# Output products laid into the last heads of two attentions, a gate/up pair ahead of each down product, modulation products spread thinner

## The chip, the cores and the metric

The kernel runs on one core of one Trainium2 chip. The metric is the device time of one execution in microseconds (us); a lower one is better. Three runs of the kernel before took 2721.72, 2729.32 and 2738.30 us, so the median is 2729.32 us. One further execution was profiled, and took 2725.89 us.

The core has a matrix engine (PE, with its weight loads shown apart as PEld), a vector engine (DVE), an activation engine (ACT), GpSimd (POOL) and a sync engine (SP), which here issues DMA transfers. Each has its own list of instructions and goes through it in order; semaphores make one wait for another.

## The reference, cut to what matters

One sequence of 512 tokens, width 1024, float32, goes through two blocks:

```python
# first block, layer 0, then layer 1
hn = modulate(rms_norm(h, norm1_g[l]), sh1, sc1)
mix = chunk_rel_attention(...)  if l == 0 else  mla_attention(...)     # 16 heads each, ends in  o @ wo
h = h + g1[:, None, :] * mix
hn = modulate(rms_norm(h, norm2_g[l]), sh2, sc2)
h = h + g2[:, None, :] * conv_ffn(hn, f_win[l], f_conv_w[l], f_conv_b[l], f_wout[l])

def conv_ffn(hn, win, conv_w, conv_b, wout):        # 1024 -> 2 x 2816 -> 1024
    y = conv_b + sum(up[:, tap:tap + S] * conv_w[tap] for tap in range(3))   # up: hn @ win, padded
    gate, val = jnp.split(y, 2, axis=-1)
    return (jax.nn.silu(gate) * val) @ wout

# second block
h = h + 0.5 * gt1 * swiglu(modulate(rmsnorm(h)), w1_gate, w1_up, w1_down)    # 2816 wide
h = h + gt2 * ((sigmoid(ga) * (ya @ w_proj_a) + sigmoid(gb) * (yb @ w_proj_b)) @ w_out)
h = h + 0.5 * gt3 * swiglu(modulate(rmsnorm(h)), w2_gate, w2_up, w2_down)
```

Every shift, scale and gate (`sh1`, `sc1`, `g1`, ...) is a column of a product silu(c) @ W + b: the "modulation". There are 184 such columns of 128 numbers.

## The kernel before, in words

The activations lie transposed: feature blocks of 128 on the partitions, 512 tokens along the free axis. `self.h` holds the residual as eight tiles of 128x512. A product of float32 accuracy is made of three matmuls in a reduced format: each operand is a high part (`wh`, `uh`) and a low part (`wl`, `ul`), and `mm3` (L328 to L330) adds high times high, high times low, low times high. A weight tile comes through `wload`: a DMA into one of four `wr` buffers, a cast on ACT (L311), a subtraction on DVE (L312). An activation is split in the same way by `split` (L341 on ACT, L342 on DVE). `gemm` takes one tile of weights and a list of split activations, and sums 3 matmuls of 512 columns for each into one bank of PSUM (three banks of tag "g", two of "s", two of "t", one of "o").

A framework's scheduler puts the instructions of each engine in an order. The order in which the code is written is its starting point; it may move a ready instruction ahead of one that it expects to wait. What it lists is what the engine carries out, one after the other.

**Attention** (`heads`, called by `block_a` and by `mla`): 16 heads, each with four query steps. A step makes scores on PE, a softmax on DVE (L477, L479, L721 or L935) and ACT (L478); two steps later it makes transposes on PE (L510) and a split of them (`pth`, `ptl`); after the fourth step the values product follows (`ps_o`, twelve matmuls). During a pair of heads, the projections of the next pair give PE something else to do; for the last heads nothing is left to project. Each finished pair of heads is written to DRAM (`oa`, L565).

**Output product** (`branch_out`): weights of a tail (`tw`), then the pairs back from DRAM and split (`pairs_back`, through two buffers "tn"), then eight blocks: weights `wo[j]` (`bwo[j]` in the second attention), a gemm over the first five pairs (15 matmuls), and on DVE `resid` (L445), which adds it to `h`. A tail over the other three pairs follows in two halves of the tokens, and the norm of the next stage with it.

**FFN** (`ffn`, used by `conv_ffn` twice and by `swiglu` twice): 22 hidden blocks in parts of 8, 8 and 3 (`PARTS`), and 3 for the tail. A hidden block is two gemms of 24 matmuls (the gate and value halves), and then work on ACT and DVE that ends in the split `hidh`, `hidl`. After each part come its eight down products: weights `fout`, a gemm over the part's hidden blocks, `resid`. In the two conv FFNs, four modulation columns are computed after each hidden block from the third on (`run_bg(4)`, `gemv`: a load of 512 KB through the same `wr` ring on SP, a multiplication with a sum on DVE, L462, and an addition, L463). There are 72 of them in each conv FFN.

Of the kernel before, what the change touches and what calls it, by code (L numbers as in the profile page):

```python
# [19 lines left out]
P = 128  # L20
# [264 lines left out]
class _K:  # L285
# [195 lines left out]

    def heads(self, pool, n, begin, lag=2):

        wait = []

# [6 lines left out]
        for h in range(n):  # L495
            probs, v, m, done = begin(h)
            pt = [pool.tile([P, 13, P], F32R, tag=t, bufs=2, name=t) for t in ("pth", "ptl")]
            for i in range(4):
                then = (lambda pt=pt, v=v, m=m, done=done: done(self.values(pt, v, m))) if i == 3 else None
                wait.append((i, probs(i), pt, then))  # L500
                if len(wait) > lag:
                    finish()
        while wait:
            finish()

    def transpose(self, i, p, pt):
# [59 lines left out]

    def pairs_back(self, dram):
        oo = []
        for p in range(8):
            if p < 7:  # L570
                t = self.tmp(tag="tn", bufs=2)
                self.nc.sync.dma_start(t, dram[p])
            else:
                t = self.o32
            oo.append(self.hl(self.gp, "u", 16, t))
        return oo


    def build(self):
# [19 lines left out]
        with self.tc.tile_pool(name="ca", bufs=1) as ca:  # L599
# [11 lines left out]
            with self.tc.tile_pool(name="pr", bufs=1) as pr:  # L611
                norm = self.conv_ffn(0, norm, m0(5), 4, lambda: self.norm_of("kv_norm_g", mk(1), mk(0)),
                                     self.rope_tables(pr))
                cact = self.c_act(ca, 1)
                norm = self.mla(norm, m1)
            self.bg = self.gemv_jobs(cact, [(j, 112, "b_ada") for j in range(112, 184)])
            norm = self.conv_ffn(1, norm, m1(5), 4, lambda: _Norm2(
                self, self.col("final_g", 0, 8), self.gain_scale(ada(1), self.col("g_ff1", 0, 8)), ada(0)))
# [30 lines left out]
    def block_a(self, cact, m0):  # L649
# [4 lines left out]
        with self.tc.tile_pool(name="pa", bufs=1) as pa:  # L654
# [75 lines left out]

            self.heads(pa, 16, begin)
            out = self.branch_out(pa, [("pth", 2), ("ptl", 2)] * 2, od, "wo", m0(2), lambda: self.norm_of("norm2_g0", m0(4), m0(3)))
        self.dump("ha", self.h)
        return out

    def branch_out(self, pool, tags, od, w, gate, mk_norm):

        tw = self.tail_weights(pool, tags, w + "t")
        oo = self.pairs_back(od)
        for j in range(8):  # L740
            x = self.wload(self.a[w][j], HEAD * P)
            self.resid(j, self.gemm(x, oo[:HEAD]), gate[:, j:j + 1])
        norm = mk_norm()
        self.tail(tw, oo[HEAD:], gate, norm)
        return norm


    def two_first(self, pf, ap, u):
# [5 lines left out]
        pss = self.gemm_halves(ws, u, "ggtt")  # L754
        return {0: pss[:2], 1: pss[2:]}

    def conv_ffn(self, l, norm, gate, nbg, mk_norm, aside=None):
# [26 lines left out]

        norm = self.ffn(hidden, f"fout{l}", gate, mk_norm)
        self.dump(f"hf{l}", self.h)
        return norm

    def ffn(self, hidden, wd, gate, mk_norm):
        with self.tc.tile_pool(name="pf", bufs=1) as pf:  # L790
            for pi, (f0, f1) in enumerate(PARTS):
# [3 lines left out]
                if pi == 2:  # L795
                    tw = self.tail_weights(pf, [("tw", 4)] * 4, wd + "t")
                    last = []
                    for f in range(f1, KF):
                        hidden(pf, f, last)
                n, g = f1 - f0, 8 // (f1 - f0)  # L800
                for j in range(8):
                    if j % g == 0:
                        w = self.wload(self.a[f"{wd}{pi}"][j // g], g * n * P)
                    self.resid(j, self.gemm(w, hid, (j % g) * n * P), gate[:, j:j + 1])
            self.run_bg(1000)
            norm = mk_norm()
# [51 lines left out]
    def mla(self, norm, m1):  # L858
        nc, a, gp = self.nc, self.a, self.gp
        with self.tc.tile_pool(name="pm", bufs=1) as pm:  # L860
# [78 lines left out]

            self.heads(pm, 16, begin)  # L940
            out = self.branch_out(pm, [("pth", 2), ("ptl", 2)] * 2, od, "bwo", m1(2), lambda: self.norm_of("norm2_g1", m1(4), m1(3)))
# [4 lines left out]
    def swiglu(self, n, norm, gt, mk_norm):  # L946
# [18 lines left out]

        out = self.ffn(hidden, f"w{n}d", hg, mk_norm)
        self.dump(f"hs{n}", self.h)
# [403 lines left out]
```

## Time and profile before

| | |
|---|---|
| three runs | 2721.72, 2729.32, 2738.30 us |
| the profiled execution | 2725.89 us |
| its span (first to last instruction) | 2724.1 us |
| PE busy | 2599.7 us, 95% |
| PEld busy | 2138.4 us, 79% |
| DVE busy | 1761.2 us, 65% |
| ACT busy | 1208.1 us, 44% |
| granted PE clock, mean | 0.981 of full |

PE is the engine that is busy nearly all the time. A matmul's busy time includes its way through the array, during which the next one has already begun; how fast PE really goes is read from the distance between the starts of two matmuls. The clock granted to PE goes between two levels, 1.2 and 2.4 GHz; the windows give its mean as a share of the higher one.

### The profile page before, as it was taken

Reading aid. Unit: us, or ns where it says so; the run is one execution under the profiler, and the core shown is the slowest. Engines: PE = TensorE matmul, PEld = TensorE weight load, DVE = VectorE, ACT = ScalarE, POOL = GpSimd, SP = SyncE. Lnnn points to the kernel's source line nnn. Section 1 sums busy time; section 2 is a strip of 40 time slices with the busy share of each in tenths; the row PEclk is TensorE's granted clock in tenths of the full one; section 3 lists DMA queues with packets and bytes.
Section 4 is the critical chain, followed back from the end, with each engine's and each line's share of the span. In section 5 each row is a group of like instructions: output and inputs, shape, how many; then the busy total and the mean of one; then the engine's idle time right before and its main releaser. Section 6 shows DMA issues by size and latency. Waiting matters only on the chain. (4 is left out here: it accounts for less than half of the span.)

```text
span 2724.1 us, 34800 instructions
## 1 busy us (share of the span) xinstructions
PE 2599.7 (95%) x12666; PEld 2138.4 (79%) x12666; DVE 1761.2 (65%) x3362; ACT 1208.1 (44%) x2119; POOL 95.2 (3%) x138
## 2 busy tenths in 40 slices
PE   7898999999898999999999999999999989999998
PEld 5776888788676888778888888887877767888887
DVE  7796896867788796958633335788365455533344
ACT  5465542334677442324622224677355434422232
POOL 1000200000000100000100001000000000100000
PEclk9999999999899999999999999999999989999999
DMA  8774376663154465745133332433257653232331
GB/s 275 208 217 132 121 236 204 227 200 114 52 140 132 138 223 173 261 163 180 45 109 93 97 116 76 119 96 97 80 171 264 228 180 124 74 98 93 101 112 43
DMA packets 146639, 395.77 MB, mean 145 GB/s; under 512 B 23954, under 2 KB 28178, under 8 KB 146468
## 3 DMA queue, kind: packets, MB, share of 16 engines
q1 hardware_dynamic: 146468, 393.55, 45.4%
q8 instruction: 100, 1.64, 0.2%
q14 instruction: 71, 0.58, 0.1%
HBM read 341.05 MB, written 26.21 MB: 135 GB/s over the span
## 5 line engine op out<-in xcount | busy, mean ns | idle before, releaser
L329 PE MATMUL ps_g<-ul,wh 128*128 128x512 f32 (+1 forms) x2156 | 835.8, 389 | 15.9 <-POOL ul L401 13.0
L328 PE MATMUL ps_g<-uh,wh 128*128 128x512 f32 (+1 forms) x2156 | 831.1, 388 | 15.7 <-ACT uh L341 10.8
L330 PE MATMUL ps_g<-uh,wl 128*128 128x512 f32 (+1 forms) x2156 | 829.4, 386 | 0.0
L311 ACT CAST wh<-wr 128x1024 fp32r<-128x1024 f32 (+3 forms) x398 | 397.5, 999 | 928.8 <-PE ps_g L329 698.5
L312 DVE TENSOR_TENSOR wl<-wr,wh 128x1024 fp32r<-128x1024 f32 (+3 forms) x398 | 462.2, 1163 | 250.2 <-ACT wh L311 238.3
L328 PEld LDWEIGHTS ps_g<-uh,wh 128*128 128x128 f32 x2156 | 408.1, 190 | 106.7 <-ACT uh L341 13.4
L329 PEld LDWEIGHTS ps_g<-ul,wh 128*128 128x128 f32 x2156 | 410.2, 190 | 100.5 <-POOL ul L401 18.2
L330 PEld LDWEIGHTS ps_g<-uh,wl 128*128 128x128 f32 x2156 | 409.4, 190 | 79.9 <-issue 2.0
L462 DVE CUSTOM_DVE_ANT_0 wr<-wr,cact 128x1024 f32<-128x1024 f32 x184 | 226.0, 1234 | 69.5 <-DMA wr<-mod 69.1
L328 PE MATMUL ps_g<-hidh,wh 128*128 128x512 f32 x608 | 241.3, 397 | 7.1 <-ACT hidh L341 7.1
L330 PE MATMUL ps_g<-hidh,wl 128*128 128x512 f32 x608 | 241.2, 397 | 0.0
L329 PE MATMUL ps_g<-hidl,wh 128*128 128x512 f32 x608 | 240.8, 396 | 0.0
L328 PEld LDWEIGHTS ps_g<-hidh,wh 128*128 128x128 f32 x608 | 115.2, 190 | 35.5 <-ACT hidh L341 8.3
L329 PEld LDWEIGHTS ps_g<-hidl,wh 128*128 128x128 f32 x608 | 115.0, 189 | 27.8 <-DVE hidl L342 0.2
L330 PEld LDWEIGHTS ps_g<-hidh,wl 128*128 128x128 f32 x608 | 115.3, 190 | 27.3
L445 DVE SCALAR_TENSOR_TENSOR h<-ps_g,mods,h 128x512 f32<-128x512 f32 (+1 forms) x112 | 73.0, 653 | 94.6 <-PE ps_g L330 94.2
L445 DVE SCALAR_TENSOR_TENSOR h<-ps_g,hg,h 128x512 f32<-128x512 f32 (+1 forms) x64 | 43.7, 683 | 127.2 <-PE ps_g L330 127.1
L478 ACT ACTIVATE p<-p,st 128x128 f32<-128x128 f32 (+1 forms) x192 | 107.4, 560 | 40.9 <-DVE st L477 40.0
L963 DVE TENSOR_TENSOR cv<-ps_g,cv 128x512 f32<-128x512 f32 x42 | 29.1, 692 | 127.8 <-PE ps_g L330 126.5
L362 POOL TENSOR_TENSOR acc<-acc,sq 128x256 f32<-128x256 f32 x42 | 34.1, 813 | 2014.5 <-ACT sq L361 1335.8
L341 ACT CAST hidh<-cv 128x512 fp32r<-128x512 f32 x88 | 54.6, 620 | 90.4 <-DVE cv L780 83.2
L398 ACT ACTIVATE uh<-tn,mods 128x256 fp32r<-128x256 f32 (+1 forms) x120 | 60.3, 519 | 65.5 <-DVE tn L394 64.8
(380 smaller groups left out, 3981.4 us busy)
## 6 DMA issues: line engine op xcount, KB each, us to landing
wr<-mod SPq DMA_DIRECT2D x184, 512.0 KB, 4.2
wr<-fin SPq DMA_DIRECT2D x88, 512.0 KB, 4.3
wr<-fout SPq DMA_DIRECT2D x32, 512.0 KB, 3.6
wr<-w1g SPq DMA_DIRECT2D x22, 512.0 KB, 3.5
wr<-w1u SPq DMA_DIRECT2D x22, 512.0 KB, 3.5
wr<-w2g SPq DMA_DIRECT2D x22, 512.0 KB, 3.6
wr<-w2u SPq DMA_DIRECT2D x22, 512.0 KB, 3.5
wr<-wqk SPq DMA_DIRECT2D x16, 512.0 KB, 4.4
```

The costliest lines, as they stand in the source:

```text
L311: nc.scalar.copy(h[:, :n], r[:, :n])
L312: nc.vector.tensor_tensor(l[:, :n], r[:, :n], h[:, :n].bitcast(F32), ALU.subtract)
L328: mm(ps, wh, xh, start=start, stop=False)
L329: mm(ps, wh, xl, start=False, stop=False)
L330: mm(ps, wl, xh, start=False, stop=stop)
L341: self.nc.scalar.copy(h, src)
L362: (eng or nc.vector).tensor_tensor(acc[:, cs], acc[:, cs], s[:, cs], ALU.add)
L398: nc.scalar.activation(h[:, cs], t, AF.Identity, bias=sh)
L445: self.nc.vector.scalar_tensor_tensor(self.h[j][:, cs], ps, g, self.h[j][:, cs], ALU.mult, ALU.add)
L462: nc.vector.tensor_tensor_reduce(w, w, cact, 1.0, 0.0, ALU.mult, ALU.add, accum_out=self.mods[:, j:j + 1])
L478: nc.scalar.activation(p[:, :n], p[:, :n], AF.Exp, bias=st[:, 0:1], scale=-1.0, accum_out=st[:, 1:2])
L963: nc.vector.tensor_tensor(t, pss[1], t, ALU.mult)
```

## The change

Three edits.

1. **Output product inside the last heads.** `heads` takes a list of jobs (`fill`) and calls one after each query step of the last two heads. The first job brings back and splits the first five pairs (now through three buffers "acc"), the next seven are blocks 0 to 6 of the output product, and the eighth block comes after the last head. `branch_out` then loads the tail's weights, brings back pairs 5 to 7, and goes on with the tail. This holds for both attentions.
2. **A pair ahead of each down product.** After parts 0 and 1 of each of the four FFNs, the two gemms of the next part's first hidden block are made (into the two "t" banks of PSUM) before the eight down products; their work on ACT and DVE stays where the next part begins.
3. **Modulation spread.** Three columns instead of four after a hidden block, and one after each of the sixteen down products of parts 0 and 1.

```diff
-    def heads(self, pool, n, begin, lag=2):
+    def heads(self, pool, n, begin, lag=2, fill=()):
...
                 wait.append((i, probs(i), pt, then))
                 if len(wait) > lag:
                     finish()
+                if h >= n - 2 and fill:
+                    fill.pop(0)()
         while wait:
             finish()
+        for f in fill:
+            f()
...
-    def pairs_back(self, dram):
+    def pairs_back(self, dram, p0, p1):
...
-                t = self.tmp(tag="tn", bufs=2)
+                t = self.tmp(tag="acc", bufs=3)
...
-                norm = self.conv_ffn(0, norm, m0(5), 4, lambda: self.norm_of("kv_norm_g", mk(1), mk(0)),
+                norm = self.conv_ffn(0, norm, m0(5), 3, lambda: self.norm_of("kv_norm_g", mk(1), mk(0)),
...
-            self.heads(pa, 16, begin)
+            self.heads(pa, 16, begin, fill=self.branch_head(od, "wo", m0(2)))
...
+    def branch_head(self, od, w, gate):
+
+        oo = []
+
+        def block(j):
+            x = self.wload(self.a[w][j], HEAD * P)
+            self.resid(j, self.gemm(x, oo), gate[:, j:j + 1])
+
+        return [lambda: oo.extend(self.pairs_back(od, 0, HEAD))] + [lambda j=j: block(j) for j in range(8)]
+
     def branch_out(self, pool, tags, od, w, gate, mk_norm):
 
         tw = self.tail_weights(pool, tags, w + "t")
-        oo = self.pairs_back(od)
-        for j in range(8):
-            x = self.wload(self.a[w][j], HEAD * P)
-            self.resid(j, self.gemm(x, oo[:HEAD]), gate[:, j:j + 1])
+        oo = self.pairs_back(od, HEAD, 8)
         norm = mk_norm()
-        self.tail(tw, oo[HEAD:], gate, norm)
+        self.tail(tw, oo, gate, norm)
...
+    def pair_early(self, first, ap, u):
+
+        def early(f):
+            first[f] = [self.gemm(w, u, tag="t") for w in [self.wload(x) for x in ap(f)]]
+
+        return early
...
+                else:
+                    early(f1)
                 n, g = f1 - f0, 8 // (f1 - f0)
                 for j in range(8):
                     if j % g == 0:
                         w = self.wload(self.a[f"{wd}{pi}"][j // g], g * n * P)
                     self.resid(j, self.gemm(w, hid, (j % g) * n * P), gate[:, j:j + 1])
+                    if pi < 2:
+                        self.run_bg(1)
```

How the order moves on the engines, at three places. In the rows `ps_s` are scores, `ps_t<-ident,p` transposes, `ps_o` values, `ps_g<-uh,wh` (or `ul`, `wl`) matmuls of a product with weights.

PE, block A, where head 15's scores begin. Before, scores and transposes follow each other with nothing between:

```order
L551 MATMUL ps_s<-k,q 128x512
L510 MATMUL ps_t<-ident,p 128x128 x2
L550 MATMUL ps_s<-k,q 128x128
L551 MATMUL ps_s<-tn,q 128x128
L550 MATMUL ps_s<-k,q 128x256
L551 MATMUL ps_s<-tn,q 128x256
L510 MATMUL ps_t<-ident,p 128x128 x3
L550 MATMUL ps_s<-k,q 128x384
L551 MATMUL ps_s<-tn,q 128x384
```

After, blocks of the output product stand between them:

```order
L328 MATMUL ps_g<-uh,wh 128x512
L329 MATMUL ps_g<-ul,wh 128x512
L330 MATMUL ps_g<-uh,wl 128x512
L555 MATMUL ps_s<-k,q 128x128
L556 MATMUL ps_s<-tn,q 128x128
L515 MATMUL ps_t<-ident,p 128x128 x3
L328 MATMUL ps_g<-uh,wh 128x512
L329 MATMUL ps_g<-ul,wh 128x512
L330 MATMUL ps_g<-uh,wl 128x512
```

Fifteen matmuls of one block now lie between the scores of one query step and those of the next, and the transposes of an earlier step follow the scores; the blocks stood before in one run behind head 15.

DVE, the same place. `ptl` is the split of the transposes, `p,st<-ps_s,b` the first softmax instruction, L721 (L726 after) the scaling. Before:

```order
L479 RECIPROCAL st<-st 128x1
L477 ISA p,st<-ps_s,b 128x384
L477 ISA st 128x1
L721 TENSOR_SCALAR p<-p,st 128x128
L342 TENSOR_TENSOR ptl<-ps_t,pth 128x3x128
L479 RECIPROCAL st<-st 128x1
L477 ISA p,st<-ps_s,b 128x512
L477 ISA st 128x1
L721 TENSOR_SCALAR p<-p,st 128x256
L342 TENSOR_TENSOR ptl<-ps_t,pth 128x4x128
```

After:

```order
L445 SCALAR_TENSOR_TENSOR h_83<-ps_g,mods,h_83 128x512
L477 ISA p,st<-ps_s,b 128x128
L477 ISA st 128x1
L312 TENSOR_TENSOR wl<-wr,wh 128x640
L479 RECIPROCAL st<-st 128x1
L342 TENSOR_TENSOR ptl<-ps_t,pth 128x3x128
L726 TENSOR_SCALAR p<-p,st 128x128
L342 TENSOR_TENSOR ul<-acc,uh 128x512
L445 SCALAR_TENSOR_TENSOR h_84<-ps_g,mods,h_84 128x512
L477 ISA p,st<-ps_s,b 128x256
```

A split of weights (`wl`), a split of a pair (`ul<-acc`) and the addition to `h` (L445) of an output block now stand between the instructions of a softmax; the addition can't begin before PE has finished its block, and the softmax instruction behind it waits for it.

SP, down products of the first conv FFN's first part. `fout` are weights of a down product, `fin` of a hidden block, `mod` of a modulation column. Before:

```order
L308 DMA wr<-fin 128x1024 x2
L461 DMA wr<-mod 128x1024 x4
L308 DMA wr<-fout 128x1024 x8
L308 DMA wr<-fin 128x1024 x2
L461 DMA wr<-mod 128x1024 x4
L308 DMA wr<-fin 128x1024 x2
```

After:

```order
L461 DMA wr<-mod 128x1024 x3
L308 DMA wr<-fin 128x1024 x2
L461 DMA wr<-mod 128x1024 x3
L308 DMA wr<-fin 128x1024 x2
L308 DMA wr<-fout 128x1024
L461 DMA wr<-mod 128x1024
L308 DMA wr<-fout 128x1024
L461 DMA wr<-mod 128x1024
L308 DMA wr<-fout 128x1024
L461 DMA wr<-mod 128x1024
```

One hidden block's `fin` now goes ahead of the `fout` loads, and a modulation load stands between each two of these; all go through the same four `wr` buffers.

## Rows read from the trace of the kernel before

**Rows 1.** The page, part 1: busy us of each engine, share of span, instructions.

```profile
PE 2599.7 (95%) x12666; PEld 2138.4 (79%) x12666; DVE 1761.2 (65%) x3362; ACT 1208.1 (44%) x2119; POOL 95.2 (3%) x138
```

**Rows 2.** Windows: stretch, its length; PE, PEld, DVE, ACT, POOL busy; granted clock; DMA.

```profile
226.40:258.00 31.60, 22.63 (x118) 16.84 (x117) 24.50 (x73) 22.82 (x56) 0.14 (x1) 0.89 0.42 122
258.00:286.00 28.00, 28.00 (x131) 23.31 (x130) 15.91 (x22) 9.05 (x12) 0.00 (x0) 1.00 0.52 174
...
537.00:548.00 11.00, 9.34 (x29) 7.47 (x30) 4.20 (x6) 2.58 (x3) 0.00 (x0) 0.69 0.25 90
```

**Rows 3.** Windows, same columns: the end of the second attention.

```profile
849.00:888.00 39.00, 32.47 (x187) 24.51 (x186) 32.34 (x104) 30.05 (x76) 0.00 (x0) 0.96 0.46 132
888.00:917.00 29.00, 29.00 (x144) 24.67 (x143) 17.95 (x25) 9.53 (x14) 0.00 (x0) 1.00 0.51 167
```

**Rows 4.** Timeline of PE, block A's end: start, duration, instruction, idle before and releaser.

```profile
226.42 0.22 PE L550 MATMUL ps_s<-k,q 128*128 128x128 f32 x1
...
236.02 0.45 PE L328 MATMUL ps_o<-pth,vsh 128*64 128x512 f32 x1 [1.65 <-ACT pth L341]
...
252.09 0.44 PE L328 MATMUL ps_o<-pth,vsh 128*64 128x512 f32 x1 [1.21 <-ACT pth L341]
...
255.49 0.80 PE L328 MATMUL ps_g<-uh,wh 128*128 128x512 f32 x1
...
284.72 0.28 PE L328 MATMUL ps_g<-uh,tw 128*128 128x256 f32 x1
```

**Rows 5.** Timeline of PE, the second attention's end.

```profile
850.48 0.41 PE L510 MATMUL ps_t<-ident,p 128*128 128x128 f32 x2
...
881.30 0.44 PE L328 MATMUL ps_o<-pth,vs 128*64 128x512 f32 x1 [1.21 <-ACT pth L341]
...
885.38 0.60 PE L328 MATMUL ps_g<-uh,wh 128*128 128x512 f32 x1
...
913.62 0.28 PE L328 MATMUL ps_g<-uh,tw 128*128 128x256 f32 x1
```

**Rows 6.** Timeline of PE, first conv FFN, end of its second part.

```profile
534.63 0.39 PE L329 MATMUL ps_g<-hidl,wh 128*128 128x512 f32 x1
538.66 0.80 PE L328 MATMUL ps_g<-hidh,wh 128*128 128x512 f32 x1 [3.64 <-ACT hidh L341]
539.26 0.63 PE L330 MATMUL ps_g<-hidh,wl 128*128 128x512 f32 x1
539.68 0.63 PE L328 MATMUL ps_g<-hidh,wh 128*128 128x512 f32 x1
...
544.60 0.40 PE L329 MATMUL ps_g<-hidl,wh 128*128 128x512 f32 x1
...
548.92 0.39 PE L330 MATMUL ps_g<-hidh,wl 128*128 128x512 f32 x1
```

**Rows 7.** Timeline of PE, second conv FFN, the same place.

```profile
1170.08 0.80 PE L328 MATMUL ps_g<-hidh,wh 128*128 128x512 f32 x1 [3.47 <-ACT hidh L341]
```

**Rows 8.** Groups by line and form: count, busy us, mean ns, idle before.

```profile
L312 DVE TENSOR_TENSOR wl<-wr,wh 128x1024 fp32r<-128x1024 f32 x334 | 408.3, 1223 | 212.5 <-ACT wh L311 201.0
...
L462 DVE CUSTOM_DVE_ANT_0 wr<-wr,cact 128x1024 f32<-128x1024 f32 x184 | 226.0, 1234 | 69.5 <-DMA wr<-mod 69.1
...
L445 DVE SCALAR_TENSOR_TENSOR h<-ps_g,mods,h 128x512 f32<-128x512 f32 x72 | 54.0, 750 | 89.4 <-PE ps_g L330 89.4
...
L312 DVE TENSOR_TENSOR wl<-wr,wh 128x640 fp32r<-128x640 f32 x32 | 26.0, 821 | 8.2 <-ACT wh L311 8.1
...
L342 DVE TENSOR_TENSOR ul<-tn,uh 128x512 fp32r<-128x512 f32 x21 | 14.2, 686 | 4.6 <-ACT uh L341 4.6
...
L341 ACT CAST uh<-tn 128x512 fp32r<-128x512 f32 x21 | 12.9, 618 | 8.3 <-DVE tn L394 4.9 <-DMA tn<-oa 2.1 <-DMA tn<-ob 1.2
```

**Rows 9.** DMA issues of the page: count, size, median us to landing.

```profile
wr<-mod SPq DMA_DIRECT2D x184, 512.0 KB, 4.2
...
wr<-fout SPq DMA_DIRECT2D x32, 512.0 KB, 3.6
```

More of the change, by code (lines that the diff above doesn't have):

```diff
@@ L480, in softmax @@
         return p, st
-    def heads(self, pool, n, begin, lag=2):
-        wait = []
+    def heads(self, pool, n, begin, lag=2, fill=()):
+        wait, fill = [], list(fill)
         def finish():
@@ L565, in pair_out @@
             self.nc.sync.dma_start(dram[p], self.o32)
-    def pairs_back(self, dram):
+    def pairs_back(self, dram, p0, p1):
         oo = []
-        for p in range(8):
+        for p in range(p0, p1):
             if p < 7:
-                t = self.tmp(tag="tn", bufs=2)
+                t = self.tmp(tag="acc", bufs=3)
                 self.nc.sync.dma_start(t, dram[p])
@@ L616, in build @@
             self.bg = self.gemv_jobs(cact, [(j, 112, "b_ada") for j in range(112, 184)])
-            norm = self.conv_ffn(1, norm, m1(5), 4, lambda: _Norm2(
+            norm = self.conv_ffn(1, norm, m1(5), 3, lambda: _Norm2(
                 self, self.col("final_g", 0, 8), self.gain_scale(ada(1), self.col("g_ff1", 0, 8)), ada(0)))
@@ L783, in hidden, with ffn @@
                 self.run_bg(nbg)
-        norm = self.ffn(hidden, f"fout{l}", gate, mk_norm)
+        norm = self.ffn(hidden, self.pair_early(first, ap, u), f"fout{l}", gate, mk_norm)
         self.dump(f"hf{l}", self.h)
         return norm
-    def ffn(self, hidden, wd, gate, mk_norm):
+    def ffn(self, hidden, early, wd, gate, mk_norm):
         with self.tc.tile_pool(name="pf", bufs=1) as pf:
@@ L938, in begin @@
                 return probs, [x[:, :, 64 * e:64 * e + 64] for x in v], 64, lambda ps: self.pair_out(pm, od, p, ps, e)
-            self.heads(pm, 16, begin)
+            self.heads(pm, 16, begin, fill=self.branch_head(od, "bwo", m1(2)))
             out = self.branch_out(pm, [("pth", 2), ("ptl", 2)] * 2, od, "bwo", m1(2), lambda: self.norm_of("norm2_g1", m1(4), m1(3)))
@@ L964, in hidden @@
             hid.append(self.hl(pf, "hid", 24, t))
-        out = self.ffn(hidden, f"w{n}d", hg, mk_norm)
+        out = self.ffn(hidden, self.pair_early(first, ap, u), f"w{n}d", hg, mk_norm)
         self.dump(f"hs{n}", self.h)
```

## The prediction

> **What bounds the kernel now.** I read the page's engine totals first. PE is busy 95% of the span, DVE 65%, ACT 44% [rows 1], so time can only come out of stretches in which PE waits or runs slowly. To find them I read PE's timeline for the distance between starts. In an undisturbed run, 19 matmuls of 512 columns lie between 544.60 and 548.92, so they start 0.227 us apart (0.445 ns a column), though each is shown as 0.39 or 0.40 us busy [rows 6]. After a long wait they start 0.42 us apart (539.26 and 539.68) [rows 6]: PE then runs at the lower of its two clock levels, and the window over that place shows a granted clock of 0.69 [rows 2].
>
> The change touches three kinds of places.
>
> Block A's end: from 226.42, the first score for which no projection is left as cover, to 284.72, the first of the unbroken tail rows, lie 58.3 us [rows 4]. The 235 matmuls that start there have 90,752 columns, which stream in 40.4 us. So 17.9 us are lost, nearly all before the output product begins at 255.49. There PE waits for the split of the transposes (1.65 and 1.21 us in the rows shown), and the window's granted clock is 0.89 [rows 2, 4].
>
> The second attention's end: from 850.48 to 913.62, 63.1 us [rows 5], 290 matmuls with 107,136 columns, 47.7 us. 15.5 us are lost, again nearly all before its output product at 885.38, and on the same split.
>
> The conv FFNs' second parts: PE reaches the down products and waits 3.64 us (first FFN) and 3.47 us (second) for the last hidden block's split [rows 6, 7], and then goes at half rate. From 534.63 to 544.60 are 10.0 us [rows 6]; the 16 matmuls that start in it would have streamed in 16 x 0.228 = 3.6 us: 6.3 us are lost. For the second FFN I take 0.2 us less by its shorter wait, 6.1 us. After the first parts, and in the two swiglus, PE's timeline shows no such wait.
>
> **The change part by part.** No arithmetic of PE goes or comes; instructions are moved.
>
> *Output product inside block A's last heads.* Seven blocks of 15 matmuls, 15 x 0.228 = 3.4 us each, come between query steps. A step's own attention is 1,920 columns on average (scores 640, transposes 320, a quarter of the values 960), 0.85 us; together 4.3 us. What DVE must do in it: the window of 226.40 to 258.00 holds 24.50 us of DVE work [rows 2] for the twelve steps of the last three heads, with the pair splits among it, so under 2.0 us a step; one weight split of 0.82 us and one addition to h of 0.75 us come on top [rows 8], 3.6 us. So DVE fits a step, without much room. Over the stretch as a whole the sum is tighter: DVE is busy 24.50 + 15.91 = 40.4 us between 226.40 and 286.00 [rows 2], and PE's columns ask for 40.4 us too. DVE's work there isn't all needed before the tail, but two engines with equal work and one fixed order each don't overlap without gaps. The bounds: all 17.9 us come back, or nothing does (the waits only change place). At the new junction behind head 15, ACT's copy of the values and its casts of tail weights, DVE's two subtractions of these and the split of the last pair (0.69 us, [rows 8]) stand ahead of the tail: an estimate of 4 us, against one product block and less as cover (3.4 us and under). 1 to 2 us of the loss stay there. For gaps on DVE, and on PE when the first pairs come back from DRAM, I leave 5 us more. Value taken: 11 us, range 6 to 14.
>
> The pairs are brought back by SP, three of them early, since "acc" has three buffers; the weights of the tail come after the blocks' own. The cast `uh` of a pair now stands ahead of a softmax's exponential on ACT. Before, the 21 casts of this form idled 2.1 us in all on loads of pairs [rows 8], which is small.
>
> *The same in the second attention.* The lost time is 15.5 us. DVE has 32.34 + 17.95 = 50.3 us of work in the 68 us from 849 to 917 [rows 3], and PE's streaming is about 52 us there (the 47.7 us above, and what lies on either side): again two nearly equal loads. Heads 12 and the beginning of 13 stay without cover, since the blocks begin in head 13 by the listed order. Value taken: 8 us, range 4 to 12.
>
> *The pair ahead of the down products.* 48 matmuls, 48 x 0.228 = 10.9 us, now stand between the second part's last gemm and its down products. The wait was 3.64 us, so the pair outlasts it three times over, and no slow clock follows. Nothing is added: the same pair is left out later. If the cover failed, it would be because the pair's own weights are late: two subtractions of 1.22 us on DVE [rows 8], behind a backlog. With three modulation products, a hidden block's DVE work falls by 1.23 us [rows 8] and two short instructions, which shrinks that backlog. Value: 5.5 us in each of the two FFNs, range 4 to 6.3. After the first parts and in the swiglus: 0, since nothing was lost there.
>
> *Modulation spread.* It takes work off DVE in the hidden stage (PE streams there for the most part, so little direct gain) and adds it to each of 32 down blocks. Such a block asks DVE for an addition (0.75 us), a weight subtraction (1.22 us) and now a product (1.23 us, all [rows 8]) with its two short instructions, some 3.4 us; PE takes 24 x 0.228 = 5.5 us. Value 0. Bounds: from a gain of 2 us (hidden stages that were a little behind) to a loss that rival C works out.
>
> The sum: 11 + 8 + 5.5 + 5.5 = 30 us. Against the profiled execution of 2725.89 us that gives 2695.9 us. The median of the three runs lies 3.4 us above that execution, and I take half of this difference: 2697.6, in round numbers **2698 us**. Ends of the terms: 6 + 4 + 4 + 4 - 2 = 16 us and 14 + 12 + 6.3 + 6.1 + 2 = 40 us, times of 2712 and 2687 us on the same base.
>
> **The rivals.**
>
> A. DVE and ACT take the place of the waits. On DVE a softmax instruction now stands behind an addition that waits for PE's block, and behind pair and weight splits that wait for a DMA. For it: DVE's 40.4 us against PE's 40.4 [rows 2, 4]. Against: two query steps, 8.6 us, lie between a softmax and its use. Then the attentions give a third of their loss, 17.9/3 + 15.5/3 = 11 us, and with the FFNs' 11 us: 2725.9 - 22 + 1.7 = 2705.5 us. The Trainium skill states a rule that makes this possible (Perfetto Trace Analysis, Tensor Engine Instruction): ACT, DVE and GpSimd are strict FIFO, unlike PE, which can pull weight loads ahead. Where it bites, the trace will show DVE idle on L445 with ready work behind it; the trace of before can't, as no addition stands among the softmaxes there.
>
> B. Only idle time comes back, and half-rate stretches remain for a reason of their own. Idle by busy time is 31.60 - 22.63 = 9.0 us in block A, 39.00 - 32.47 = 6.5 us in the second attention [rows 2, 3], 3.64 and 3.47 us in the FFNs [rows 6, 7]: 22.6 us at most, 2705 us. Against: the slow stretch stands right behind the wait [rows 6]. The Trainium skill (Trainium Kernel Development and Optimization, Performance Expectations) calls matmul busy time a bad metric, because matmuls are pipelined; by that rule B's cap is none. The trace agrees on the rule itself, with 0.39 us busy against 0.227 us from start to start.
>
> C. Slower: the down products wait for weights. A `fout` load lands 3.6 us after its issue, a `mod` load 4.2 us [rows 9], and the products L462 idled 69.1 us on their loads, 0.38 us for each of 184 [rows 8]. In the down stage the loads now alternate in one ring of four, and a buffer comes free only when DVE has done with it: if DVE waits for a `mod`, the next block's weights wait behind it. If each of the 32 blocks in the conv FFNs came 1 us late, that is 32 us and cancels the gain; from there on the change is slower: at 1.5 us late, 48 - 30 = 18 us lost, 2746 us. Against: two loads for 5.5 us are no higher rate than the six for 10.9 us (48 matmuls) of a hidden block before, and a lead of about two buffers, 11 us, stands against 4.2 us of landing, a cast, and a subtraction of 1.22 us.
>
> D. The change doesn't do what it says where it counts: the waits in the heads come from the scheduler's list, which shifts in earlier heads too, and what is gained in the last heads is lost there. Then only the FFN terms are left, 2725.9 - 11 + 1.7 = 2716.6 us.
>
> **How the numbers follow.** Forecast (2687 to 2702) 0.55; A and B together 0.30 (A 0.22, B 0.08), 2702 to 2711; D 0.10, 2711 to 2722; C 0.05. The range takes in the forecast's lower end with some room for a larger gain, and reaches up through A and B into D: 2682 to 2712. A measurement of this kernel can tell 0.5%, 13.6 us, from no change: faster means below 2715.7 us. Forecast, A, B and a third of D lie there: 0.88. The rest of D and a C that stops near 1 us: 0.08. C beyond: 0.04.
>
> **What would show it.** In the changed kernel's profile: block A from the first score without cover to the tail in 46 to 49 us where 58.3 stood; no wait above 1 us on the split of transposes there, and a granted clock near 1.00; no gap before the first `hidh` matmul of a second part, but 48 starts of a gate/up pair (`ps_t`) 0.23 us apart; in the down products starts 0.23 us apart throughout. Wrong if PE's waits in the heads are now on `wh`, `uh` or `wl` (A), if starts stay 0.42 us apart without a wait before them (B), or if the down stage shows a wait for `wh` or `wl` in every block (C).

## The result and the profile after

The changed kernel took 2696.31 us (median of 4 runs, 2693.35 to 2701.35) against 2729.23 us before (median of 4). The ratio is 0.9877, with a 95% interval of 0.986 to 0.9894: 33 us faster. 2698 us were forecast. The profiled execution of it took 2697.24 us, 28.7 us less than that of before. Timed a second time it gave 2692.13 us, ratio 0.9864 (0.9846 to 0.9882).

The page's engine totals, which answer to [rows 1] (busy us, share of the span, instructions):

```profile
PE 2587.6 (96%) x12666; PEld 2125.6 (79%) x12666; DVE 1756.0 (65%) x3362; ACT 1204.9 (45%) x2118; POOL 90.8 (3%) x138
```

PE is busy 12 us less and the span is 28.6 us shorter; the instructions are as many, but for one load of a table on ACT (2118 for 2119).

The ends of the two attentions as windows (the columns of [rows 2]):

```profile
216.50:262.80 46.30, 43.67 (x230) 34.84 (x230) 32.98 (x84) 26.20 (x59) 0.14 (x1) 1.00 0.47 136
829.50:883.50 54.00, 52.30 (x286) 42.00 (x285) 40.67 (x110) 32.06 (x76) 0.00 (x0) 1.00 0.50 152
```

The first answers to the two windows of block A [rows 2], the second to those of the second attention [rows 3]. The granted clock is 1.00 where it was 0.89 and 0.96, and PE is busy in nearly all of each. DVE has the least slack in the second: 40.67 of 54 us.

PE's timeline at block A's end (start, duration, instruction, idle before and releaser), which answers to [rows 4]:

```profile
216.56 0.22 PE L555 MATMUL ps_s<-k,q 128*128 128x128 f32 x1
...
223.88 0.50 PE L555 MATMUL ps_s<-k,q 128*128 128x128 f32 x2 [1.01 <-DMA k<-k]
...
227.58 0.50 PE L556 MATMUL ps_s<-k,q 128*128 128x128 f32 x2 [0.81 <-DMA k<-k]
...
258.90 0.45 PE L328 MATMUL ps_o<-pth,vsh 128*64 128x512 f32 x1 [0.56 <-ACT pth L341]
...
260.07 0.45 PE L329 MATMUL ps_o<-ptl,vsh 128*64 128x512 f32 x1
...
262.86 0.28 PE L328 MATMUL ps_g<-uh,tw 128*128 128x256 f32 x1
```

From the first score that no projection covers to the unbroken tail are 46.3 us, where 58.3 stood (with six matmuls fewer in it, 229 for 235, which stream in 0.7 us). The longest wait for the transposes' split is 0.56 us, behind head 15; two of 1.01 and 0.81 us are on the stacked keys of head 14, which arrive by DMA. The second attention's end, which answers to [rows 5]:

```profile
829.51 0.41 PE L515 MATMUL ps_t<-ident,p 128*128 128x128 f32 x2
...
879.59 0.45 PE L328 MATMUL ps_o<-pth,vs 128*64 128x512 f32 x1 [0.88 <-ACT pth L341]
...
881.48 0.40 PE L329 MATMUL ps_o<-ptl,vs 128*64 128x512 f32 x1
...
883.52 0.28 PE L328 MATMUL ps_g<-uh,tw 128*128 128x256 f32 x1
```

54.0 us, where 63.1 stood (again with six matmuls fewer); the one large wait is again behind the last head (0.88 us), and from there to the low part at 881.48 seven matmuls of an output block fill the gap.

The first conv FFN's second part, which answers to [rows 6]:

```profile
509.64 0.39 PE L328 MATMUL ps_t<-uh,wh 128*128 128x512 f32 x1
...
520.30 0.39 PE L330 MATMUL ps_t<-uh,wl 128*128 128x512 f32 x1
520.52 0.39 PE L328 MATMUL ps_g<-hidh,wh 128*128 128x512 f32 x1
520.75 0.39 PE L329 MATMUL ps_g<-hidl,wh 128*128 128x512 f32 x1
```

The starts of the gate/up pair's 48 matmuls go from 509.64 to 520.30, and the first down product starts 0.22 us after the last: no wait and no half rate.

Groups by line and form, which answer to [rows 8] (count, busy us, mean ns, idle before):

```profile
L462 DVE CUSTOM_DVE_ANT_0 wr<-wr,cact 128x1024 f32<-128x1024 f32 x184 | 226.8, 1235 | 111.8 <-DMA wr<-mod 110.8
...
L445 DVE SCALAR_TENSOR_TENSOR h<-ps_g,mods,h 128x512 f32<-128x512 f32 x72 | 53.8, 748 | 32.1 <-PE ps_g L330 32.1
...
L342 DVE TENSOR_TENSOR ul<-acc,uh 128x512 fp32r<-128x512 f32 x18 | 12.3, 687 | 0.8 <-ACT uh L341 0.5
...
L341 ACT CAST uh<-acc 128x512 fp32r<-128x512 f32 x18 | 11.0, 618 | 3.7 <-DMA acc<-oa 2.6 <-DMA acc<-ob 1.1
```

DVE's idle time ahead of additions to h falls from 89.4 to 32.1 us. Nearly all of that is in the conv FFNs (52.9 us before, 4.7 after), where modulation products now fill the time. Its idle time on loads of modulation columns rises from 69.1 to 110.8 us.

**Where the time went.** For each trace I summed, over PE's matmuls, the distance to the next start minus the streaming time (0.2285 us for 512 columns, 0.174 for 384, 0.119 for 256, 0.058 for 128): the us lost in a stretch. The streaming times are distances between starts in undisturbed runs of these traces. The row in brackets overlaps the two above it: it begins where the forecast's stretch of block A begins, and has the same 377 matmuls in every kernel. Two traces of a kernel stand with a comma; the other kernels are those of the experiments below.

| us lost | before | pairs in acc only | pair ahead only | spread only | blocks in heads only | changed kernel | changed, no spread |
|---|---|---|---|---|---|---|---|
| start to head 0's values | 26.7, 25.1 | 22.2 | 26.4 | 23.5 | 22.8 | 20.6, 23.6 | 21.5, 23.4 |
| to head 12's values | 22.2, 22.3 | 24.2 | 22.6 | 22.5 | 19.3 | 17.5, 20.9 | 21.4, 20.0 |
| to block A's tail's end | 16.8, 16.4 | 11.1 | 17.8 | 17.0 | 5.8 | 6.6, 6.3 | 6.8, 6.8 |
| (first uncovered score to block A's tail's end) | 18.8, 18.3 | 16.7 | 19.7 | 18.9 | 6.7 | 7.6, 7.3 | 7.7, 7.7 |
| first conv FFN, second part | 6.6, 7.5 | 8.8 | 0.7 | 7.5 | 8.2 | 0.6, 0.3 | 1.7, 1.5 |
| its third part | 0.2, 0.2 | 0.2 | 1.1 | 0.2 | 0.2 | 5.3, 3.2 | 0.6, 0.2 |
| second attention, head 10 to its tail's end | 16.4, 17.0 | 16.8 | 16.8 | 16.6 | 8.2 | 8.8, 8.7 | 8.6, 8.7 |
| second conv FFN, second part | 8.7, 8.7 | 8.4 | 1.1 | 4.2 | 7.2 | 3.6, 0.2 | 0.3, 3.0 |
| its third part | 1.7, 1.7 | 1.7 | 1.8 | 1.7 | 1.7 | 6.5, 2.9 | 1.8, 1.8 |

By the means of two traces: the attentions' ends gave 10.2 and 8.0 us. The conv FFNs' second parts gave 6.6 and 6.8 us, of which 4.1 and 3.0 us were lost again in their third parts. Before head 12 of block A, where the forecast had nothing, 6.9 us went. Together 31.4 us less is lost; the spans differ by 31.0 us.

The third part's new waits (PE, first conv FFN):

```profile
581.77 0.47 PE L328 MATMUL ps_g<-uh,wh 128*128 128x512 f32 x1 [1.25 <-DVE cv L796]
...
587.72 0.47 PE L328 MATMUL ps_g<-uh,wh 128*128 128x512 f32 x1 [0.22 <-DVE cv L796]
...
595.17 0.47 PE L328 MATMUL ps_g<-uh,wh 128*128 128x512 f32 x1 [1.75 <-ACT cv L794]
```

### The profile page after: what moved, and what is told of

Its sections match the earlier page's. It is cut to its first block, busy times and chain, and to the rows that moved or that the text cites. A ratio compares the mean times of both kernels' runs of the same rounds, so it can differ in the third digit from the quotient of the medians.

```text
span 2695.5 us, 34803 instructions
## 1 busy us (share of the span) xinstructions
PE 2587.6 (96%) x12666; PEld 2125.6 (79%) x12666; DVE 1756.0 (65%) x3362; ACT 1204.9 (45%) x2118; POOL 90.8 (3%) x138
## 5 line engine op out<-in xcount | busy, mean ns | idle before, releaser
L328 PE MATMUL ps_g<-uh,wh 128*128 128x512 f32 (+1 forms) x2028 | 779.6, 388 | 23.5 <-ACT uh L341 11.6
L329 PE MATMUL ps_g<-ul,wh 128*128 128x512 f32 (+1 forms) x2028 | 785.1, 388 | 16.0 <-POOL ul L401 13.7
L330 PE MATMUL ps_g<-uh,wl 128*128 128x512 f32 (+1 forms) x2028 | 778.5, 385 | 0.0
L328 PEld LDWEIGHTS ps_g<-uh,wh 128*128 128x128 f32 x2028 | 382.1, 190 | 111.4 <-ACT uh L341 14.3
L329 PEld LDWEIGHTS ps_g<-ul,wh 128*128 128x128 f32 x2028 | 384.5, 190 | 95.7 <-POOL ul L401 20.0
L330 PEld LDWEIGHTS ps_g<-uh,wl 128*128 128x128 f32 x2028 | 384.1, 190 | 74.8 <-issue 2.0
L462 DVE CUSTOM_DVE_ANT_0 wr<-wr,cact 128x1024 f32<-128x1024 f32 x184 | 226.8, 1235 | 111.8 <-DMA wr<-mod 110.8
L328 PEld LDWEIGHTS ps_g<-hidh,wh 128*128 128x128 f32 x608 | 113.8, 187 | 28.6 <-ACT wh L311 1.2
L445 DVE SCALAR_TENSOR_TENSOR h<-ps_g,hg,h 128x512 f32<-128x512 f32 (+1 forms) x64 | 43.7, 683 | 125.8 <-PE ps_g L330 125.7
L445 DVE SCALAR_TENSOR_TENSOR h<-ps_g,mods,h 128x512 f32<-128x512 f32 (+1 forms) x112 | 72.8, 652 | 38.5 <-PE ps_g L330 38.3
```

The costliest lines, as they stand in the source:

```text
L328: mm(ps, wh, xh, start=start, stop=False)
L329: mm(ps, wh, xl, start=False, stop=False)
L330: mm(ps, wl, xh, start=False, stop=stop)
L445: self.nc.vector.scalar_tensor_tensor(self.h[j][:, cs], ps, g, self.h[j][:, cs], ALU.mult, ALU.add)
L462: nc.vector.tensor_tensor_reduce(w, w, cact, 1.0, 0.0, ALU.mult, ALU.add, accum_out=self.mods[:, j:j + 1])
```

## The experiments

Times are medians; ratios are to the kernel before in the same session. A ratio isn't exactly the quotient of two medians, so of two near kernels the one with the higher median can have the lower ratio.

**The kernel before once more** (no edit). 

> The kernel before, unchanged, as a second trace of it. Theory 1 (the 6 us that the changed kernel was ahead by before the first head's values are chance: how soon loads land): PE's first wait on the stacked keys is anywhere from 1 to 4 us, the first head's values end anywhere from 100 to 107 us, and the time stays within 0.3% of 2729 us. Theory 2 (they come from the change): the wait is again 3.4 us within 0.3 us and the values end at 106 us.

2726.7 us, ratio 0.9985 (0.9971 to 0.9999). The interval leaves out 1 although nothing was changed, so a difference of 4 us between two such sets of runs shows nothing yet. PE's first wait on the stacked keys (`k` tiles, put together from parts by DMA moves between partitions), in before, its repeat, the pair-only kernel and the changed kernel, from each timeline of PE:

```profile
87.91 0.77 PE L550 MATMUL ps_s<-k,q 128*128 128x128 f32 x2 [3.45 <-DMA k<-k]
```

```profile
87.61 0.47 PE L550 MATMUL ps_s<-k,q 128*128 128x128 f32 x2 [3.63 <-DMA k<-k]
...
88.55 0.63 PE L328 MATMUL ps_g<-uh,wh 128*128 128x512 f32 x1
```

```profile
89.04 0.77 PE L555 MATMUL ps_s<-k,q 128*128 128x128 f32 x2 [5.09 <-DMA k<-k]
```

```profile
84.55 0.47 PE L555 MATMUL ps_s<-k,q 128*128 128x128 f32 x2 [1.49 <-DMA k<-k]
```

The repeat has the long wait again, near what theory 2 gave (3.63 us, values at 104.8 us). But the pair-only kernel, with block A's instructions as before, waits 5.09 us there, so the size moves by itself.

**Blocks in the heads only.** 

> The output product inside the last heads of both attentions, without the pair ahead of the down products and with the modulation as before. Theory 1: 12 us in block A's last heads and 7.5 us in the second attention, 2709 us, with the waits of 3.6 and 3.5 us at the conv FFNs' second parts as before and no wait in their third parts. Theory 2 (the change also speeds the early heads by 9 us): 2700 us, and the first head's values end near 100 us.

```diff
-                else:
-                    early(f1)
...
-                    if pi < 2:
-                        self.run_bg(1)
...
-                norm = self.conv_ffn(0, norm, m0(5), 3, lambda: ...
+                norm = self.conv_ffn(0, norm, m0(5), 4, lambda: ...
```

(against the changed kernel). 2704.52 us, ratio 0.9900 (0.9881 to 0.9918), midway between the theories. The wait at the first conv FFN's second part is there as before, on PE:

```profile
523.56 0.79 PE L328 MATMUL ps_g<-hidh,wh 128*128 128x512 f32 x1 [3.61 <-ACT hidh L341]
```

No wait in the third parts. The ends of the attentions lose 10.8 and 8.5 us less than the kernel before, the early heads 6.1 us less.

**Pair ahead only.** 

> The gate/up pair ahead of the down products alone, modulation as before (four columns a hidden block, none beside the down products). Theory 1 (the new waits in the third parts come because the pair puts PE one hidden block, 11 us, ahead of DVE): the 3.6 and 3.5 us waits of the second parts go, and waits in the third parts appear, 4 us or more in each conv FFN; net 0 to 5 us faster. Rival (the new waits come from the modulation beside the down products): no wait in the third parts, and 12 us faster.

The kernel before with `early(f1)` ahead of the down products. 2713.89 us, ratio 0.9922 (0.9895 to 0.995). The waits of the second parts are gone, and in the third parts there is none above 0.59 us: theory 1 falls. In the conv FFNs 13 us less are lost, which fits the rival's numbers (the four runs lie between 2706.42 and 2720.92 us); the next run tests its reason.

**Spread only.** 

> The modulation spread alone (three columns a hidden block, one beside each down product of the first two parts), no pair ahead. Theory 1: no wait in the third parts, the waits at the second parts shrink to under 2 us by the lighter hidden stage, 3 to 8 us faster. Rival (the modulation beside the down products makes the third parts wait): waits of about 4 us in the third part of each conv FFN, and no faster.

The kernel before with `run_bg(1)` beside down products and 3 for 4. 2729.52 us, ratio 0.9995 (0.9983 to 1.0008): no gain. The third parts run without a wait, so the rival falls too; and the second part's wait did not shrink in the first FFN (PE):

```profile
545.19 1.22 PE L328 MATMUL ps_g<-hidh,wh 128*128 128x512 f32 x2 [5.60 <-ACT hidh L341]
```

In the second FFN it was 3.67 us, for 3.47 before. So neither edit makes the third part wait by itself.

**Both, without the spread.** 

> The change without its third edit: output product in the last heads and pair ahead of the down products, modulation as before (four columns a hidden block, none beside the down products). The runs so far: neither the pair alone nor the spread alone makes the conv FFNs' third parts wait, the two together do (4 to 5 us each). Theory (the third part waits only where pair and spread meet): no waits there, and the second FFN's second part 2 us shorter, so 2685 us, some 11 us faster than the changed kernel. Rival (the wait comes from the pair together with the output product's shift, or is chance): third parts wait about 4 us again, 2696 us.

```diff
-                    if pi < 2:
-                        self.run_bg(1)
```

(and 4 for 3, against the changed kernel). 2692.49 us, ratio 0.9865 (0.9844 to 0.9886). The third parts' waits are gone, as the theory said, but not its 11 us: the time is 4 us under the first timing of the changed kernel.

**No modulation in the third part.** 

> The changed kernel with two modulation columns beside each down product of the first two parts and none in the third part (three a hidden block before). Theory D (DVE's load in the third part makes PE wait for its PSUM banks): both third parts run without a wait, 2688 us. Theory L (tail weights' casts stand ahead of the work on the hidden block in ACT's list, and their loads queue behind modulation loads on SP): the wait before the first gemm of the third part's second block stays at 1 us or more, as two modulation loads for each down product now stand ahead of the tail weights; only the later one goes; 2692 us or slower.

```diff
-            if f > 1:
+            if 1 < f < 16:
                 self.run_bg(nbg)
...
                     if pi < 2:
-                        self.run_bg(1)
+                        self.run_bg(2)
```

2697.25 us, ratio 0.9886 (0.9869 to 0.9904). The third parts lose 0.2 and 1.8 us, as before the change: theory D in that, though not in its 2688 us, and L's remaining wait didn't show. But the second parts now lose 4.8 and 6.2 us, with waits among their hidden blocks (PE, second conv FFN):

```profile
1073.11 0.47 PE L328 MATMUL ps_g<-uh,wh 128*128 128x512 f32 x1 [0.40 <-DVE cv L796]
...
1081.89 0.47 PE L328 MATMUL ps_g<-uh,wh 128*128 128x512 f32 x1 [3.08 <-DVE mods L463]
```

The waits moved with the columns; no time was won.

**Tail weights late.** 

> The changed kernel with the loads and splits of an FFN's tail weights moved behind the last hidden block (in all four FFNs). Theory L (their casts and late loads hold up ACT's list): the waits in the conv FFNs' third parts go, 8 us faster than the changed kernel if the tail doesn't wait, 2688 us; the tail may wait for its weights instead, up to 2 us in each of four FFNs. Theory D (DVE's load of the third part as a whole): waits of 2 us or more stay in the third part of each conv FFN, 2695 us.

```diff
-                    tw = self.tail_weights(pf, [("tw", 4)] * 4, wd + "t")
                     last = []
                     for f in range(f1, KF):
                         hidden(pf, f, last)
+                    tw = self.tail_weights(pf, [("tw", 4)] * 4, wd + "t")
```

2695.06 us, ratio 0.987 (0.9851 to 0.989). The third parts still lose 4.2 and 4.3 us: theory L falls.

**The changed kernel and the one without spread, side by side.** 

> The changed kernel unchanged, for a second trace and beside the next one. Four kernels without the output product in the heads lost 46 to 49 us (by starts against streaming) up to head 12 of block A, five with it 38 to 43 us; the changed kernel's 38 was the lowest. If that was chance in part: 40 to 43 us here, and 2697 us. If it is the changed kernel's own: 38 us again.

> The change without its third edit once more, beside the changed kernel. Theory (by the columns that are left when the second part's hidden blocks are done, 22 with the spread against 16 without, the spread costs 8 to 12 us in the conv FFNs): 2686 to 2692 us, 6 us or more faster than the changed kernel beside it. Rival (the two differ by chance): within 3 us.

2692.13 us, ratio 0.9864 (0.9846 to 0.9882), and 2694.12 us, ratio 0.9858 (0.9838 to 0.9878). The changed kernel's early heads lost 44.5 us this time: its 38.1 was chance in part. The spread's cost can't be told from nothing by time; the means of all runs are 2694.5 us with it (8 runs) and 2691.9 us without (10 runs). Over the whole span the traces lose 225.4 us with it and 224.4 us without: what the third parts lose by it is nearly made up elsewhere.

**Pairs in three buffers only.** 

> The kernel before with one word changed: pairs come back through the three buffers acc instead of the two tn, nothing else moved. Theory (heads 1 to 12 of block A gain 3 us because the keys' last tile, which also lives in tn, no longer shares it with pairs): 18 to 20 us lost in heads 1 to 12 where the kernel before loses 22, and 3 us faster. Rival (they gain because the list of instructions changes by the output product's blocks themselves): 22 us lost, as before, and no faster.

```diff
-                t = self.tmp(tag="tn", bufs=2)
+                t = self.tmp(tag="acc", bufs=3)
```

(in `pairs_back` of the kernel before). 2719.39 us, ratio 0.9962 (0.9948 to 0.9976): 10 us faster, though heads 1 to 12 lost 24.2 us, so the theory falls and the rival's "no faster" too. The traces place 7.6 us of the gain: 3.7 us before head 0's values, 1.7 us from there to the first uncovered score, 1.9 us from that score to block A's tail's end (16.7 us lost, not 18.6), and little behind it. From head 12's values on, 11.1 us are lost instead of 16.6, but most of that difference only changed its row: a wait of 2.02 us and a slow stretch now lie ahead of these values. DVE's splits of the seven pairs, before and with this edit (shortest, middle and longest in ns; first and last start):

```profile
L342 DVE TENSOR_TENSOR ul<-tn,uh x7: 674/687/693, 235.5 to 258.9; 128x512 fp32r<-128x512 f32 x7
```

```profile
L342 DVE TENSOR_TENSOR ul<-acc,uh x7: 671/684/692, 216.4 to 241.8; 128x512 fp32r<-128x512 f32 x7
```

With "tn", which also holds the keys' last tile (`k.append(self.tmp(dt=F32R, tag="tn", bufs=2))` in `project`), the first pair is split at 235.5 us, and all seven behind the first uncovered score (226.4); with "acc" the first is at 216.4, and three of the seven stand ahead of that score (220.4). The edit changes both which tiles share the buffers and how many buffers there are; no run separates these.

**Blocks in the heads, pairs in the old buffers.** 

> The first two edits (output product in the last heads, pair ahead of the down products), with pairs coming back through the two buffers tn as before instead of the three acc. By starts against streaming, block A from head 12's values to the tail's end lost 16.8 us before, 11.1 with acc alone, 6.3 to 6.8 with acc and the blocks in the heads. Theory 1 (two separate gains, 5.7 for the buffers and 4.5 for the blocks): 12 to 13 us lost there, 2698 us. Theory 2 (one gain: either relieves the same waits, so the blocks alone do most of it): 8 us or less lost there, 2694 us.

2705.35 us, ratio 0.9902 (0.9889 to 0.9916), slower than both theories by time. Block A's end lost 8.4 us, near theory 2. But from the first uncovered score it lost 10.5 us, where blocks and buffers together lose 7.7, buffers alone 16.7 and the kernel before 18.6: by that measure the two gains nearly add up (8 and 1.9 us, 10.9 together), as theory 1 has it. So this run doesn't decide between the theories. The second attention lost 12.4 us against 8.7 with "acc", and the start of block A lost 25.6. The splits in block A stand late again:

```profile
L342 DVE TENSOR_TENSOR ul<-tn,uh x7: 681/691/694, 233.6 to 256.4; 128x512 fp32r<-128x512 f32 x7
```

By the medians the buffers are worth some 12 us beside the blocks. The traces show 5 us of it (229.4 us lost in all, for 224.4), and the traced execution was the fastest of its five (2700.40 us).

**Blocks wider apart in the second attention.** 

> The first two edits, and in the second attention the nine jobs go one to every second query step of the last four heads instead of every step of the last two. The second attention from head 10 to its tail's end loses 8.7 us in every kernel with the blocks in two heads, 16.8 without. Theory (heads 12 and 13, which have no projections to cover them either, hold most of the rest): 4 to 6 us lost there, 3 to 4 us faster, 2689 us. Rival (what is left is the junction behind the last head and the tail): 8.5 us or more again, 2692 us or slower.

```diff
-                if h >= n - 2 and fill:
+                if h >= n - last and i % every == 0 and fill:
...
-... fill=self.branch_head(od, "bwo", m1(2)))
+... fill=self.branch_head(od, "bwo", m1(2)), last=4, every=2)
```

2691.47 us, ratio 0.9862 (0.9847 to 0.9878), not distinguishable from the kernel without it. The second attention lost 7.2 us, between the theory's 6 and the rival's 8.5. No version beat the changed kernel by a margin that could be measured.

## Why the prediction was right, and where it was not

The time was 1.7 us from the forecast, but the terms did not all come as written.

*Output product in block A, 11 us:* right in size. From the first uncovered score to the tail's end 11.1 us less are lost (18.6 before, 7.4 after, by the means of two traces); the table's row from head 12's values has 10.2, and the 12.0 us by which the forecast's stretch shrank hold 0.7 us of work that left it. One step of the working had the cause incomplete. The forecast put the whole of it on cover for PE and mentioned the buffers in passing (`since "acc" has three buffers`). Blocks in the old buffers took 8 us off that stretch, the buffers alone 1.9 and both 10.9 to 11.1. That the buffers act by taking pair splits of 0.69 us out of DVE's list of the uncovered heads is argued from the times of the splits.

*Second attention, 8 us:* right (8.0 by lost time; the stretch shrank by 9.1, of which 0.7 is work that left it). Buffers alone did nothing there (16.8 us lost), but without them the blocks leave 12.4 us.

*Pair ahead, 11 us in both FFNs:* the mechanism was right and the size low, 13.4 us. (For the first FFN the forecast counted 16 matmuls where 15 start, 0.2 us.) Then the step "Modulation spread. Value 0" failed. The sum per down block (3.4 of 5.5 us on DVE) was sound, and the down products do run without waits. What it left out is when the 72 columns are done. Before, 14 hidden blocks had done 56 when the second part's down products began; with three each and eight beside the first part's down products it is 42 + 8 = 50. So 22 columns were left for that point on instead of 16, beside a PE that the pair had put further ahead. In the stretch of the second part's down products and of the third part behind it, DVE's windows of the changed kernel:

```profile
520.00:564.00 44.00, 44.00 (x196) 36.44 (x195) 32.95 (x56) 11.30 (x13) 0.00 (x0) 1.00 0.68 216
564.00:608.00 44.00, 40.78 (x178) 32.82 (x178) 35.27 (x57) 17.26 (x22) 0.00 (x0) 1.00 0.74 244
```

and of the same kernel without the spread:

```profile
526.60:570.60 44.00, 44.00 (x196) 36.41 (x194) 28.46 (x45) 10.14 (x12) 0.00 (x0) 1.00 0.55 179
570.60:614.60 44.00, 44.00 (x196) 36.44 (x195) 35.60 (x55) 19.80 (x25) 0.00 (x0) 1.00 0.70 231
```

4.2 us more DVE work (32.95 + 35.27 against 28.46 + 35.60), and PE busy for only 40.78 us of the third part. DVE isn't full, so load alone isn't the wait; the rows point to order. The wait at 581.77 is for a bank of PSUM that PE had filled by 569.5. ACT's timeline, and SP's:

```profile
576.40 0.83 ACT L311 CAST tw<-wr 128x768 fp32r<-128x768 f32 x1 [8.65 <-DMA wr<-fout0t]
577.14 1.04 ACT L311 CAST wh<-wr 128x1024 fp32r<-128x1024 f32 x1
578.09 0.77 ACT L794 ACTIVATE cv<-ps_g,par 128x512 f32<-128x512 f32 x1
...
590.10 0.78 ACT L794 ACTIVATE cv<-ps_g,par 128x512 f32<-128x512 f32 x1
...
594.34 0.77 ACT L794 ACTIVATE cv<-ps_g,par 128x512 f32<-128x512 f32 x1
```

```profile
565.35 6.27 SPq L461 DMA_DIRECT2D wr<-mod  x3
572.62 5.96 SPq L308 DMA_DIRECT2D wr<-fout0t  x4
```

ACT reads that bank only at 578.09. Ahead of the reading it has a cast of tail weights, which idled 8.65 us on a `fout0t` load, and SP issued this load behind three modulation loads in the shared ring. In the pair-only kernel ACT has the same reading ahead of the cast, and PE doesn't wait there:

```profile
591.90 0.77 ACT L797 ACTIVATE cv<-ps_g,par 128x512 f32<-128x512 f32 x1
...
595.80 0.84 ACT L311 CAST tw<-wr 128x768 fp32r<-128x768 f32 x1 [3.13 <-DMA wr<-fout0t]
```

By the rule of the Trainium skill that ACT and DVE are strict FIFO (Perfetto Trace Analysis, Tensor Engine Instruction), a ready reading of the bank can't pass the cast; the trace agrees here, with a reading some 8 us after the bank was full and 1.25 us of PE's wait. At 595.17 the list of DVE holds the bank, with a modulation product (593.13) ahead of the last reading of it (594.28):

```profile
592.41 0.74 DVE L795 SCALAR_TENSOR_TENSOR cv<-ps_g,par,cv 128x511 f32<-128x511 f32 x1
593.07 0.15 DVE L463 TENSOR_TENSOR mods<-mods,par 128x1 f32<-128x1 f32 x1
593.13 1.22 DVE L462 CUSTOM_DVE_ANT_0 wr<-wr,cact 128x1024 f32<-128x1024 f32 x1
594.28 0.08 DVE L462 DVE_READ_ACCUMULATOR2_ANT mods<- 128x1 f32 x1
594.28 0.74 DVE L796 SCALAR_TENSOR_TENSOR cv<-ps_g,par,cv 128x510 f32<-128x510 f32 x1
```

The profile names ACT's reading of 594.34 for this wait, but that reading is of the next bank: with three banks in turn, PE needs the one that ACT had read at 590.10. So the first wait is rival C's mechanism, a load late in the ring, and the second the order on DVE; together the third parts' waits cost about 7 us, and the down blocks, where rival C put them, ran without one. In the second trace of the changed kernel this FFN's waits sit elsewhere (1.12 us at 598.40 and 1.25 us at 631.28, both behind DVE), so the rows tell how such a wait comes about, not which one comes. With the tail weights later in the lists, 4.2 us were lost there all the same.

What is shown by experiment: neither the spread nor the pair gives these waits alone, without the spread the whole change has no wait there, and the waits move with the columns. No run has the spread and the output product without the pair; that the pair is the other half is argued, and so is that the ring and the lists, and not DVE's load, decide the size.

*Rival A* came on DVE, but not in the time. In the last heads DVE does idle ahead of an addition with a softmax instruction behind it, up to 3.05 us in block A and 3.17 us in the second attention:

```profile
247.97 0.75 DVE L445 SCALAR_TENSOR_TENSOR h<-ps_g,mods,h 128x512 f32<-128x512 f32 x1 [3.05 <-PE ps_g L330]
248.64 0.55 DVE L477 CUSTOM_DVE_ANT_0 p<-ps_s,b 128x384 f32<-128x384 f32 x1
```

PE had a block to work on meanwhile, and none of its waits in these heads is on `wh`, `uh` or `wl`. *Rival B* is ruled out: the three places gave 10.2 + 8.0 + 13.4 = 31.6 us, more than the 22.6 us that were idle. *Rival D* had a point in reverse: the early heads did shift, in the good direction.

*What wasn't forecast:* 6.9 us before head 12. Some of it is chance (head 0 to 12 of the changed kernel: 38.1 and 44.5 us lost). The part before head 0's values has every engine's list unchanged, yet the kernels with "acc" lost 20.6 to 24.0 us there (9 traces) and those with "tn" 23.5 to 26.7 (5 traces). Why stays open. Without these 6.9 us the forecast's own terms come to 24.5 us instead of 30: the total was right by two errors of opposite sign, which is luck.

## What to carry to other kernels

Where background work shares buffers and an engine's fixed order with work that PE waits for, count how much of it is left at the point where PE starts to run ahead; a thinner spread may only make it later. When a change also swaps a buffer, cost the swap by itself: here it gave 10 us by time, of which the traces place 1.9 us where it was thought to act. Look for lost time in the distance between starts, not only in idle time, and begin and end a stretch where the work is the same in both kernels: a mark inside the stretch that moves carries loss from one row into another.

## What the runs showed of the hardware

With the same list of instructions on every engine up to there, PE's first wait for the stacked keys was 1.49 to 5.09 us in four executions. The last DMA move of these keys landed 3.12 us after its issue in the changed kernel, 5.32 and 5.45 us in the two executions of the kernel before, and 7.58 us in the pair-only kernel.

After each of the three waits of over 3 us the granted clock was 0.50, the lower level, in the second microsecond behind the wait; after the one of 1.49 us it stayed at 1.00. It had fallen before the wait's end after 3.45 and 5.09 us (0.77 us for the first two matmuls). After the wait of 3.63 us it fell only behind the first ones (0.47 us for these, and 0.63 us for 512 columns at 88.55), so the length of the wait alone didn't decide when.
